# T5 bias sums of a two-layer decoder trunk on one core: nine packed sets of key groups in five breaks of the matmul row, in place of twelve sets in twelve breaks

## The chip, the core and the metric

The kernel runs on one core of one Trainium2 chip. The metric is the device time of one execution in microseconds (us), the median of three runs. TensorE (PE) does the matmuls, VectorE (DVE) and ScalarE (ACT) the elementwise work, GpSimd (POOL) a few small steps, and SyncE (SP) issues the weight DMAs. Each engine works through its own queue in order, and semaphores let one engine wait for another.

## The reference, cut to what matters

The program is a decoder trunk of two layers for 256 tokens of width 1024, in float32. Layer 0 is multi-head latent attention and layer 1 block-sparse attention with 8 heads; since there are only 256 tokens, layer 1 is plain causal attention over one block of 256 keys. Each attention is followed by a squared-ReLU MLP of width 4096. Layer 1 adds a bias that depends on the distance of query and key alone:

```python
def rel_bias(pq, pk):
    return table_h[h_i4, t5_bucket(pq - pk)].astype(jnp.float32)
...
lg_own = (jnp.einsum('bhqd,bhtd->bhqt', qi, k_own).astype(jnp.float32) * scale
          + rel_bias(pq4, pos_own[:, None, None, :]))
causal = (own * MOBA_BLOCK + t_ids)[None, :] <= q_idx[:, None]
parts.append(jnp.where(causal, lg_own, -jnp.inf))
```

Only pairs with the key not after the query count. For query tile 0 (queries 0 to 127) these are keys 0 to 127, for query tile 1 (queries 128 to 255) keys 0 to 255.

## The kernel before

**Matmul rows.** A float32 weight is split on the chip into a high and a low part (`wh` by an ACT cast, line 169, and `wl` by a DVE subtraction, line 178), and so are activations, and each product is three fp32r matmuls (`mm3`, line 87). The MLP of layer 0 runs two passes `r`; in each, places 0 to 7 (`first`) make hidden values and places 8 to 15 (`d` = 0 to 7) the output chunks. Every place is a chain of 48 matmuls of 256 columns into one PSUM bank. In this text places are counted through both passes, 0 to 31; pass 2 begins at 16 and its output chunks at 24. After place 31 come the projections of layer 1, whose first one, k0, goes through the input chunks k = 0 to 7 in order, six matmuls of 512 columns each, and needs the normalised input `hTh`, `hTl` of chunk k.

**The end of a pass-2 output chunk.** DVE scales the PSUM sum (line 976), POOL adds the residual `x` (line 1041; DVE for the last chunk), ACT makes `hTh` (line 609) and DVE `hTl` (line 611). Between these stand `wh` and `wl` of later weight units. All of it is in program order.

**Bias sums.** The bias is a sum over 32 thresholds: a step matrix `st` (is the query at least the key plus the threshold?), times a table of differences `parts3`. A `BiasBlock` handles a set of 32 keys of one query tile: `steps` is one DVE comparison that makes `st` in bf16 (line 1017), `sums` is eight bf16 matmuls with 96 columns into two PSUM banks, and `add` is six DVE additions (line 1034) that bring the sums to `bias`, the first of three on the causal mask `bias0` (the program's name for it is `mask`). There are twelve sets.

**What sets the order.** A hand-written list `fillers` names a place for each `steps` and each `add`; they go onto DVE's queue at the end of that place, ahead of the scaling in an output chunk. `inside` names the place whose matmul chain a `sums` breaks, five matmuls before its end. Set i has its comparison at place 2i+6 and its break and its additions at 2i+9, so breaks stand at 9, 11, ... 31. After a break the next chain begins with a matmul of 258 columns (`wider`). PSUM banks are taken in rotation from eight (`ps`, line 71). `bias_tables` at place 5 prepares the comparison's inputs; in the same place POOL finishes a sum of squares `ssum` (lines 301 and 306), which PE reads inside place 6.

Of the kernel before, what the change touches and what calls it, by code (L numbers as in the profile page):

```python
# [15 lines left out]
OP = mybir.AluOpType  # L16
AX = mybir.AxisListType

P = 128
# [7 lines left out]
H = 8  # L27
# [26 lines left out]
NPAIR = DFF // (2 * P * NR)  # L54
# [6 lines left out]
def trunk(ctx: ExitStack, tc: tile.TileContext, A, out):  # L61
    nc = tc.nc
# [8 lines left out]
    def ps():  # L71
        return psum.tile([P, 512], F32, name="ps", tag="ps")
# [5 lines left out]
    def t2(*shape):  # L78
        return work.tile([P, *shape], F32, name="t2", tag="t2")
# [4 lines left out]
    def mm(o, a, b, start, stop):  # L84
        nc.tensor.matmul(o, a, b, start=start, stop=stop)  # L85
# [21 lines left out]
    def other_type(i, f):  # L107
        def run():
            f()
            moved[0] = False  # L110
        return i, run
# [113 lines left out]
    for k in range(KD):  # L225
        if k > 1:
            load_one()
        if k < 4 or k % 2 == 0:
            n = 1 if k < 4 else 2
# [25 lines left out]
    bias0 = mask.rearrange("p a b -> p (a b)")  # L255
# [7 lines left out]
    def gain(name, i=0):  # L263
        return gains[:, GOFF[name][0] + i:GOFF[name][0] + i + 1]
# [21 lines left out]
    class SumSquares:  # L286


        def __init__(self):
            self.tot = work.tile([P, 2, S], F32, name="ssum", tag="ssum", bufs=1)  # L290
            self.prev = None

        def add(self, b, on_pool=False):
            sq = t2(2, S)
            xs = x[:, 2 * b:2 * b + 2]
            if on_pool:
                nc.gpsimd.tensor_mul(sq, xs, xs)
            else:
                nc.scalar.activation(sq, xs, AF.Square)
            if self.prev is not None:  # L300
                nc.gpsimd.tensor_add(self.tot, self.prev, sq)
                sq = self.tot
            self.prev = sq
# [532 lines left out]
    m = t2(NT, 2, PE_D)  # L836
# [13 lines left out]
    for o, a, b in rope_halves(m[:, :, 0], m[:, :, 1]):  # L850
        a, b = (i[:, :, None, :].to_broadcast([P, NT, 2, HALF]) for i in (a, b))
# [136 lines left out]
    bias = bias_pool.tile([P, H, 3 * P], F32)  # L988
    steps_q = bias_pool.tile([P, S], F32)
    steps_k = bias_pool.tile([P, S // 4], F32)  # L990
    parts3 = bias_pool.tile([P, 3 * 4 * H], BF16)

    def bias_tables():
        nc.vector.tensor_copy(steps_q, pos_row)
        nc.vector.tensor_copy(steps_k, pos_k4)
        nc.vector.tensor_scalar(steps_k, steps_k, gain("thr"), None, op0=OP.add)
        delta = bias_pool.tile([P, 4 * H], F32, name="delta")
        nc.vector.tensor_sub(delta, tprev.rearrange("p a b -> p (a b)"), tcur.rearrange("p a b -> p (a b)"))
        rest = delta
        for i in range(3):  # L1000
            pt = parts3[:, i * 4 * H:(i + 1) * 4 * H]
            nc.vector.tensor_copy(pt, rest)
            if i < 2:
                nxt = bias_pool.tile([P, 4 * H], F32, name=f"rest{i}")
                nc.vector.tensor_sub(nxt, rest, pt)
                rest = nxt

    class BiasBlock:


        def __init__(self, blk):
            self.t, self.k0 = (0, 32 * blk) if blk < 4 else (1, 32 * (blk - 4))

        def steps(self):
            t, k0 = self.t, self.k0
            self.st = bias_pool.tile([P, 8, P], BF16, name="st", tag="st", bufs=2)
            nc.vector.tensor_tensor(self.st, steps_q[:, None, t * P:(t + 1) * P].to_broadcast([P, 8, P]),
                                    steps_k[:, k0 // 4:k0 // 4 + 8, None].to_broadcast([P, 8, P]), op=OP.is_ge)

        def sums(self):  # L1020
            self.pb = [ps() for _ in range(2)]
            for h in range(2):
                for kk in range(4):
                    mm(self.pb[h][:, kk * 96:(kk + 1) * 96], self.st[:, 4 * h + kk], parts3, True, True)

        def add(self):
            col = self.k0 if self.t == 0 else P + self.k0
            for h in range(2):
                pb = self.pb[h]
                dst = bias[:, :, col + 16 * h:col + 16 * (h + 1)]  # L1030
                src = pb[:, :384].rearrange("p (k i g h) -> p i h k g", i=3, g=4, h=H)
                for i in range(3):
                    old = dst if i else bias0[:, None, col + 16 * h:col + 16 * (h + 1)].to_broadcast([P, H, 16])
                    nc.vector.tensor_tensor(dst.rearrange("p h (k g) -> p h k g", g=4), src[:, i],  # L1034
                                            old.rearrange("p h (k g) -> p h k g", g=4), op=OP.add)

    sums1 = [None]

# [11 lines left out]
        nc.vector.tensor_add(y, o, x[:, d])  # L1050
        (nc.sync if d == KD - 1 else nc.gpsimd).dma_start(out[:, d], y)

    blocks = [BiasBlock(i) for i in range(12)]
    inside = {}
    fillers = [((0, 1), table_loads), ((0, 5), bias_tables)]
    for i, b in enumerate(blocks):

        steps, place = (divmod(2 * i + g, 2 * NPAIR) for g in (6, 9))
        fillers += [(steps, b.steps), (place, b.add)]
        inside[place] = other_type(0, b.sums)  # L1060
    mlp(0, M0, fillers, inside, finish0)


# [150 lines left out]
```

## Time and profile before

| | |
|---|---|
| median of 3 runs | 564.68 us (564.36 to 564.85) |
| the profiled execution, its own time | 564.54 us |
| its span, first to last instruction | 562.7 us |
| PE busy | 554.5 us (99%) |
| DVE busy | 396.4 us (70%) |
| ACT busy | 302.8 us (54%) |
| POOL busy | 94.6 us (17%) |
| mean granted TensorE clock | 0.997 |

The profile is of one execution. Busy time of PE counts a matmul from start to modelled end, and matmuls overlap, so a full PE says only that work was always queued; the pace is read from the starts. The timeline gives the start, the duration and the idle time before an instruction with what ended it.

### The profile page before, as it was taken

Reading aid. Unit: us, or ns where it says so; the run is one execution under the profiler, and the core shown is the slowest. Engines: PE = TensorE matmul, PEld = TensorE weight load, DVE = VectorE, ACT = ScalarE, POOL = GpSimd, SP = SyncE. Lnnn points to the kernel's source line nnn. Section 1 sums busy time; section 2 is a strip of 40 time slices with the busy share of each in tenths; the row PEclk is TensorE's granted clock in tenths of the full one; section 3 lists DMA queues with packets and bytes.
Section 4 is the critical chain, followed back from the end, with each engine's and each line's share of the span. In section 5 each row is a group of like instructions: output and inputs, shape, how many; then the busy total and the mean of one; then the engine's idle time right before and its main releaser. Section 6 shows DMA issues by size and latency. Waiting matters only on the chain.

```text
span 562.7 us, 10806 instructions
## 1 busy us (share of the span) xinstructions
PE 554.5 (99%) x4346; PEld 527.3 (94%) x4346; DVE 396.4 (70%) x654; ACT 302.8 (54%) x495; POOL 94.6 (17%) x105
## 2 busy tenths in 40 slices
PE   8999999999999999999989999999999999999997
PEld 6878999999999999999868888999999999999997
DVE  5997777778987598766678466676876753877630
ACT  6989675665433356343455556646765332655420
POOL 4892100040232000011124100000130211000100
PEclk9999999999999999999989999999999999999999
DMA  8833444686675366544454553453775764575810
GB/s 299 296 123 118 146 139 158 187 280 190 188 223 189 112 217 196 176 155 157 152 182 123 186 191 115 147 181 113 230 224 181 251 201 150 159 219 185 265 45 29
DMA packets 29186, 99.57 MB, mean 177 GB/s; under 512 B 3824, under 2 KB 4720, under 8 KB 29136
## 3 DMA queue, kind: packets, MB, share of 16 engines
q1 hardware_dynamic: 28656, 97.94, 54.1%
q0 software_dynamic: 336, 0.92, 0.4%
q8 instruction: 34, 0.56, 0.4%
q14 instruction: 16, 0.13, 0.1%
q10 hardware_dynamic: 144, 0.02, 0.0%
HBM read 97.82 MB, written 1.05 MB: 176 GB/s over the span
## 4 chain that ended last, share of the span: by engine, by line
PE 95%; DVE 2%; DMA 1%; SPq 1%; issue 1%; POOL 0%; ACT 0%; DVEq 0%
PE ps L85 92%; PE ps L372 1%; PE ps L596 1%; DMA rowp<-in_rowp 1%; DVE wl L178 1%; SPq L158 0%; SPq L230 0%; DVE bias L1034 0%; POOL ang L393 0%; DVE hTl L280 0%; PE ps L512 0%; ACT wh L169 0%; POOL posf L391 0%; ACT hTh L609 0%; DVE x L1041 0%
## 5 line engine op out<-in xcount | busy, mean ns | idle before, releaser
L178 DVE TENSOR_TENSOR wl<-raw,wh 128x1024 fp32r<-128x1024 f32 x177 | 217.0, 1241 | 37.6 <-ACT wh L169 37.0
L169 ACT CAST wh<-raw 128x1024 fp32r<-128x1024 f32 x177 | 182.7, 1047 | 72.2 <-PE ps L85 53.6
L85 PE MATMUL ps<-a,wh 128*128 128x256 f32 x1024 | 175.3, 276 | 0.0
L85 PEld LDWEIGHTS ps<-a,wh 128*128 128x128 f32 x1024 | 154.4, 188 | 0.0
L85 PE MATMUL ps<-a,wl 128*128 128x256 f32 x512 | 142.1, 277 | 0.0
L85 PE MATMUL ps<-hTl,wh 128*128 128x256 f32 x512 | 141.7, 277 | 0.0
L85 PE MATMUL ps<-hTh,wl 128*128 128x256 f32 x512 | 141.7, 277 | 0.0
L85 PE MATMUL ps<-hTh,wh 128*128 128x256 f32 x512 | 141.3, 276 | 0.0
L85 PEld LDWEIGHTS ps<-hTl,wh 128*128 128x128 f32 x512 | 96.1, 188 | 0.1
L85 PEld LDWEIGHTS ps<-hTh,wh 128*128 128x128 f32 x512 | 96.1, 188 | 0.1
L85 PEld LDWEIGHTS ps<-a,wl 128*128 128x128 f32 x512 | 96.1, 188 | 0.0
L85 PEld LDWEIGHTS ps<-hTh,wl 128*128 128x128 f32 x512 | 96.1, 188 | 0.0
L930 ACT ACTIVATE t<-ps 128x512 f32<-128x512 f32 (+1 forms) x34 | 19.5, 572 | 67.5 <-PE ps L85 67.5
L85 PE MATMUL ps<-wh,hTh 128*128 128x512 f32 (+2 forms) x128 | 46.9, 392 | 3.7 <-ACT hTh L609 2.4
L85 PE MATMUL ps<-aT,wh 128*128 128x256 f32 (+1 forms) x256 | 50.4, 288 | 0.0
L932 DVE SCALAR_TENSOR_TENSOR t<-ps,t 128x512 f32<-128x512 f32 (+1 forms) x34 | 22.4, 659 | 38.4 <-ACT t L930 38.0
L85 PE MATMUL ps<-wl,hTh 128*128 128x512 f32 (+2 forms) x128 | 45.9, 384 | 0.2 <-DVE wl L178 0.2
L85 PE MATMUL ps<-wh,hTl 128*128 128x512 f32 (+2 forms) x128 | 45.7, 383 | 0.0
L85 PEld LDWEIGHTS ps<-aT,wh 128*128 128x128 f32 x256 | 40.3, 188 | 0.2
L609 ACT ACTIVATE hTh<-x,gains 128x256 fp32r<-128x256 f32 x24 | 12.2, 510 | 47.9 <-POOL x L1041 29.7
L85 PE MATMUL ps<-aT,wl 128*128 128x256 f32 x128 | 35.6, 278 | 0.0
L978 POOL TENSOR_TENSOR x<-t,x 128x256 f32<-128x256 f32 x16 | 19.4, 1211 | 93.4 <-DVE t L976 93.4
(166 smaller groups left out, 634.7 us busy)
## 6 DMA issues: line engine op xcount, KB each, us to landing
raw<-in_w_in_mlp SPq DMA_DIRECT2D x64, 512.0 KB, 4.1
raw<-in_w_out_mlp SPq DMA_DIRECT2D x64, 512.0 KB, 4.3
raw<-in_w_qkv SPq DMA_DIRECT2D x24, 512.0 KB, 4.2
raw<-in_w_u SPq DMA_DIRECT2D x8, 512.0 KB, 5.9
win<-in_w_in SPq DMA_DIRECT2D x8, 352.0 KB, 5.3
raw<-in_w_o0a SPq DMA_DIRECT2D x4, 512.0 KB, 3.6
raw<-in_w_o0b SPq DMA_DIRECT2D x4, 512.0 KB, 3.6
raw<-in_w_o1a SPq DMA_DIRECT2D x4, 512.0 KB, 3.8
```

Of the source, the lines that this page charges most:

```text
L85: nc.tensor.matmul(o, a, b, start=start, stop=stop)
L169: (eng.copy if eng is nc.scalar else eng.tensor_copy)(his[i][:, :w], raws[i][:, :w])
L178: eng.tensor_sub(los[i][:, :w], raws[i][:, :w], f32(his[i][:, :w]))
L372: nc.tensor.transpose(pt[:, i * P:(i + 1) * P], yf[:, i * P:(i + 1) * P], ident)
L596: nc.tensor.transpose(pt[:, i * P:(i + 1) * P], self.p[:, i * P:(i + 1) * P], ident)
L609: nc.scalar.activation(hTh[:, k], x[:, k], AF.Copy, scale=gain(gname, k))
L930: nc.scalar.activation(rl, src, AF.Relu)
L932: nc.vector.scalar_tensor_tensor(sq, src, 0.0, rl, op0=OP.max, op1=OP.mult)
L978: nc.gpsimd.tensor_add(x[:, d], y, x[:, d])
```

## The change

The six sets that hold a block on the causal diagonal need only some of their queries: of keys 96 to 127 in tile 0 the queries 96 to 127, and so on. The change packs two such sets into one `st` along the query columns: 32 columns of the one and 96 of the other, or 64 and 64. Three packed sets and six whole ones remain. A packed set has two comparisons (over fewer columns) and two groups of six additions, one for each part; the part that moves to other partitions writes 32 or 64 rows. Its rows that no sum reaches are filled from the mask by three POOL copies in `bias_tables`. Two sets share a break, so breaks stand at places 9, 14, 19, 24 and 29, with sixteen bf16 matmuls in the first four and eight in the last. Comparisons stand at 6, 7, 11, 12, 16, 17, 21, 22 and 26, groups of additions at 9, 10, 11, 14, 15, 16, 19, 20, 21, 24, 25 and 29.

```diff
     def bias_tables():
+        for q, k in ((96, 96), (64, 2 * P + 64), (96, 2 * P + 96)):
+            nc.gpsimd.tensor_copy(bias[:q, :, k:k + 32], bias0[:q, None, k:k + 32].to_broadcast([q, H, 32]))
         nc.vector.tensor_copy(steps_q, pos_row)
...
-        def __init__(self, blk):
-            self.t, self.k0 = (0, 32 * blk) if blk < 4 else (1, 32 * (blk - 4))
+        def __init__(self, *parts):
+            self.parts = [(slice(m, m + P - q0), t, k0, q0) for m, t, k0, q0 in parts]
...
+            for m, t, k0, q0 in self.parts:
+                n = P - q0
+                nc.vector.tensor_tensor(self.st[:, :, m],
+                                        steps_q[:, None, t * P + q0:(t + 1) * P].to_broadcast([P, 8, n]),
+                                        steps_k[:, k0 // 4:k0 // 4 + 8, None].to_broadcast([P, 8, n]), op=OP.is_ge)
...
+        def add(self, part):
+            m, t, k0, q0 = part
+            col = k0 if t == 0 else P + k0
+
+            if m.start == q0:
+                m, q0 = slice(0, P), 0
...
-    blocks = [BiasBlock(i) for i in range(12)]
+    whole = [BiasBlock((0, *p, 0)) for p in ((0, 0), (1, 0), (1, 32), (1, 64), (1, 96), (1, 128))]
+    packed = [BiasBlock((0, 0, 96, 96), (32, 0, 32, 32)), BiasBlock((0, 1, 224, 96), (32, 1, 160, 32)),
+              BiasBlock((0, 1, 192, 64), (64, 0, 64, 64))]
+    pairs = [(whole[i], packed[i]) for i in range(3)] + [(whole[3], whole[4]), (whole[5],)]
...
-        steps, place = (divmod(2 * i + g, 2 * NPAIR) for g in (6, 9))
-        fillers += [(steps, b.steps), (place, b.add)]
-        inside[place] = other_type(0, b.sums)
+    for i, bs in enumerate(pairs):
+        at = 5 * i + 9
+        place = divmod(at, 2 * NPAIR)
...
+        fillers += [(divmod(at - 3 + j, 2 * NPAIR), b.steps) for j, b in enumerate(bs)]
+        fillers += [(divmod(at + j, 2 * NPAIR), f) for j, f in enumerate(f for b in bs for f in b.adds())]
+        inside[place] = other_type(0, sums)
```

DVE's queue at the end of pass 2, from `hTl` of output chunk 5 to the residual of chunk 7 (`t` is the scaled chunk, `x` the residual); before:

```order
L611 SCALAR_TENSOR_TENSOR hTl<-x,gains,hTh 128x256
L178 TENSOR_TENSOR wl<-raw,wh 128x1024 x2
L976 TENSOR_TENSOR t_3617<-ps,scale 128x256
L611 SCALAR_TENSOR_TENSOR hTl<-x,gains,hTh 128x256
L178 TENSOR_TENSOR wl<-raw,wh 128x1024 x2
L1034 TENSOR_TENSOR bias<-ps,mask 128x8x16
L1034 TENSOR_TENSOR bias<-ps,bias 128x8x16 x2
L1034 TENSOR_TENSOR bias<-ps,mask 128x8x16
L1034 TENSOR_TENSOR bias<-ps,bias 128x8x16 x2
L976 TENSOR_TENSOR t_3699<-ps,scale 128x256
L1041 TENSOR_TENSOR x<-t_3699,x 128x256
```

The same place in the changed kernel:

```order
L611 SCALAR_TENSOR_TENSOR hTl<-x,gains,hTh 128x256
L178 TENSOR_TENSOR wl<-raw,wh 128x1024 x2
L976 TENSOR_TENSOR t_3603<-ps,scale 128x256
L611 SCALAR_TENSOR_TENSOR hTl<-x,gains,hTh 128x256
L178 TENSOR_TENSOR wl<-raw,wh 128x1024 x2
L976 TENSOR_TENSOR t_3669<-ps,scale 128x256
L1054 TENSOR_TENSOR x<-t_3669,x 128x256
```

The six additions ahead of the last chunk's scaling have left this place.

DVE's queue where the output chunks of pass 2 begin (`a` is the last hidden value), before:

```order
L940 TENSOR_TENSOR a_1322<-t_3081,a_1321 128x512
L178 TENSOR_TENSOR wl<-raw,wh 128x1024 x2
L1034 TENSOR_TENSOR bias<-ps,mask 128x8x16
L1034 TENSOR_TENSOR bias<-ps,bias 128x8x16 x2
L1034 TENSOR_TENSOR bias<-ps,mask 128x8x16
L1034 TENSOR_TENSOR bias<-ps,bias 128x8x16 x2
L178 TENSOR_TENSOR wl<-raw,wh 128x1024
L1017 TENSOR_TENSOR st<-steps_q,steps_k 128x1024
L976 TENSOR_TENSOR t_3160<-ps,scale 128x256
```

The same place in the changed kernel:

```order
L940 TENSOR_TENSOR a_1322<-t_3077,a_1321 128x512
L178 TENSOR_TENSOR wl<-raw,wh 128x1024 x3
L1044 TENSOR_TENSOR bias<-ps,mask 128x8x16
L1044 TENSOR_TENSOR bias<-ps,bias 128x8x16 x2
L1044 TENSOR_TENSOR bias<-ps,mask 128x8x16
L1044 TENSOR_TENSOR bias<-ps,bias 128x8x16 x2
L976 TENSOR_TENSOR t_3174<-ps,scale 128x256
```

Here the additions moved from place 23 to place 24, and the comparison of place 24 is gone.

POOL's queue around place 5, one piece of the difference (the sum of squares, which PE reads in place 6):

```order
 L301 TENSOR_TENSOR ssum<-ssum,t_1618 128x512
 L301 TENSOR_TENSOR ssum<-ssum,t_1688 128x512
+L996 COPY bias<-mask 96x8x32
+L996 COPY bias<-mask 64x8x32
+L996 COPY bias<-mask 96x8x32
 L306 TENSOR_TENSOR ssum<-ssum 128x256
```

The three copies stand ahead of the last step of the sum.

## Rows read from the trace of the kernel before

**Rows 1.** The page: busy time of the engines, and the chain of work that ended last, by engine.

```profile
PE 554.5 (99%) x4346; PEld 527.3 (94%) x4346; DVE 396.4 (70%) x654; ACT 302.8 (54%) x495; POOL 94.6 (17%) x105
...
PE 95%; DVE 2%; DMA 1%; SPq 1%; issue 1%; POOL 0%; ACT 0%; DVEq 0%
```

**Rows 2.** The waits of PE: for whom, us in total, times, longest.

```profile
PE ps L85 <- ACT hTh L609: 2.4, 1, 2.4
PE ps L85 <- DVE wh L446: 1.1, 1, 1.1
...
PE ps L85 <- DVE wl L178: 0.2, 1, 0.2
```

**Rows 3.** The timeline of PE around the break at place 9 and at the next one (start, duration, operation, count).

```profile
147.57 0.39 PE L85 MATMUL ps<-a,wh 128*128 128x256 f32 x2
147.81 0.51 PE L85 MATMUL ps<-parts,st 128*128 128x96 bf16 x8
148.14 0.37 PE L85 MATMUL ps<-a,wl 128*128 128x256 f32 x1
148.34 0.40 PE L85 MATMUL ps<-a,wh 128*128 128x256 f32 x2
...
148.94 0.28 PE L85 MATMUL ps<-a,wl 128*128 128x256 f32 x1
...
149.28 0.28 PE L85 MATMUL ps<-a,wl 128*128 128x256 f32 x1
...
159.15 0.51 PE L85 MATMUL ps<-parts,st 128*128 128x96 bf16 x8
```

**Rows 4.** The instructions on the tile `st`: count, shortest, median and longest duration in ns, first and last start.

```profile
L85 PE MATMUL ps<-parts,st x96: 206/206/217, 147.8 to 272.9; 128*128 128x96 bf16 x96
```

**Rows 5.** The timeline of PE in projection k0, where it waits for chunk 7; 13 matmuls start from 283.11 to 290.17, and the next at 290.60.

```profile
282.41 0.40 PE L85 MATMUL ps<-wl,hTh 128*128 128x512 f32 x1
...
283.11 0.39 PE L85 MATMUL ps<-wl,hTh 128*128 128x512 f32 x1
285.87 0.50 PE L85 MATMUL ps<-wh,hTh 128*128 128x512 f32 x1 [2.36 <-ACT hTh L609]
...
290.17 0.59 PE L85 MATMUL ps<-wl,hTh 128*128 128x512 f32 x1
290.60 0.40 PE L85 MATMUL ps<-wh,hTh 128*128 128x512 f32 x1
```

**Rows 6.** The view by windows around it: us, busy time (count) of PE, PEld, DVE, ACT and POOL, granted TensorE clock, DMA share, GB/s.

```profile
280.00:283.00 3.00, 3.00 (x15) 2.41 (x14) 2.56 (x3) 1.34 (x2) 0.00 (x0) 1.00 0.48 145
...
286.00:290.50 4.50, 4.48 (x12) 3.35 (x13) 3.52 (x4) 4.50 (x6) 2.90 (x2) 0.63 0.20 48
290.50:295.00 4.50, 4.50 (x22) 3.58 (x21) 2.36 (x4) 1.65 (x3) 0.00 (x0) 0.99 0.77 270
```

**Rows 7.** The timeline of DVE from the scaling of output chunk 6 to `hTl` of chunk 7.

```profile
277.67 0.41 DVE L976 TENSOR_TENSOR t<-ps,scale 128x256 f32<-128x256 f32 x1
...
280.42 2.36 DVE L178 TENSOR_TENSOR wl<-raw,wh 128x1024 fp32r<-128x1024 f32 x2 [0.46 <-ACT wh L169]
282.70 0.28 DVE L1034 TENSOR_TENSOR bias<-ps,mask 128x128 f32<-128x128 f32 x1
...
284.40 0.41 DVE L976 TENSOR_TENSOR t<-ps,scale 128x256 f32<-128x256 f32 x1
284.85 0.43 DVE L1041 TENSOR_TENSOR x<-t,x 128x256 f32<-128x256 f32 x1
285.85 0.48 DVE L611 SCALAR_TENSOR_TENSOR hTl<-x,gains,hTh 128x256 fp32r<-128x256 f32 x1 [0.58 <-ACT hTh L609]
```

**Rows 8.** Groups of DVE's instructions between the scaling of chunk 0 and that of chunk 7, 238.1 to 284.3 us: count | busy us, mean ns | idle us before them, and who ended it.

```profile
L1034 DVE TENSOR_TENSOR bias<-ps,bias 128x128 f32<-128x128 f32 x16 | 4.7, 291 | 0.6
L611 DVE SCALAR_TENSOR_TENSOR hTl<-x,gains,hTh 128x256 fp32r<-128x256 f32 x7 | 3.4, 484 | 10.2 <-ACT hTh L609 10.2
...
L1017 DVE TENSOR_TENSOR st<-steps_q,steps_k 128x1024 bf16<-128x1024 f32 x2 | 2.4, 1214 | 0.0
L1034 DVE TENSOR_TENSOR bias<-ps,mask 128x128 f32<-128x128 f32 x8 | 2.3, 281 | 0.0
```

**Rows 9.** The timeline of DVE from the additions of place 23 to the scaling of chunk 0 (place 24).

```profile
233.64 0.28 DVE L1034 TENSOR_TENSOR bias<-ps,mask 128x128 f32<-128x128 f32 x1
...
235.34 1.22 DVE L178 TENSOR_TENSOR wl<-raw,wh 128x1024 fp32r<-128x1024 f32 x1
236.47 1.22 DVE L1017 TENSOR_TENSOR st<-steps_q,steps_k 128x1024 bf16<-128x1024 f32 x1
237.60 0.42 DVE L976 TENSOR_TENSOR t<-ps,scale 128x256 f32<-128x256 f32 x1
```

**Rows 10.** The timeline of POOL: the last step of the sum of squares, and the residual of chunk 0 in pass 1.

```profile
126.67 0.74 POOL L306 TENSOR_TENSOR ssum<-ssum 128x256 f32<-128x256 f32 x1
147.81 1.65 POOL L978 TENSOR_TENSOR x<-t,x 128x256 f32<-128x256 f32 x1 [20.40 <-DVE t L976]
```

**Rows 11.** The timeline of PE in place 6, where it reads the sum of squares.

```profile
131.14 0.59 PE L85 MATMUL ps<-ssum,ones 128*128 128x256 f32 x2
```

**Rows 12.** Groups of POOL's instructions over the whole span, columns as in rows 8.

```profile
L415 POOL TENSOR_SCALAR rr<-rr 128x64 f32<-128x64 f32 x1 | 0.9, 893 | 0.1
...
L748 POOL MEMSET kpT<- 128x256 f32 x2 | 0.6, 312 | 0.0
```

More of the change, by code (lines that the diff above doesn't have):

```diff
@@ L1008, in trunk @@
     class BiasBlock:
-        def __init__(self, blk):
-            self.t, self.k0 = (0, 32 * blk) if blk < 4 else (1, 32 * (blk - 4))
+        def __init__(self, *parts):
+            self.parts = [(slice(m, m + P - q0), t, k0, q0) for m, t, k0, q0 in parts]
         def steps(self):
-            t, k0 = self.t, self.k0
             self.st = bias_pool.tile([P, 8, P], BF16, name="st", tag="st", bufs=2)
-            nc.vector.tensor_tensor(self.st, steps_q[:, None, t * P:(t + 1) * P].to_broadcast([P, 8, P]),
-                                    steps_k[:, k0 // 4:k0 // 4 + 8, None].to_broadcast([P, 8, P]), op=OP.is_ge)
+            for m, t, k0, q0 in self.parts:
[3 more added lines that the diff above has]
+                                        steps_k[:, k0 // 4:k0 // 4 + 8, None].to_broadcast([P, 8, n]), op=OP.is_ge)
         def sums(self):
@@ L1024, in sums, with adds @@
                     mm(self.pb[h][:, kk * 96:(kk + 1) * 96], self.st[:, 4 * h + kk], parts3, True, True)
-        def add(self):
-            col = self.k0 if self.t == 0 else P + self.k0
+        def add(self, part):
[3 more added lines that the diff above has]
+                m, q0 = slice(0, P), 0
             for h in range(2):
-                pb = self.pb[h]
-                dst = bias[:, :, col + 16 * h:col + 16 * (h + 1)]
-                src = pb[:, :384].rearrange("p (k i g h) -> p i h k g", i=3, g=4, h=H)
+                cols = slice(col + 16 * h, col + 16 * (h + 1))
+                dst = bias[q0:, :, cols]
+                src = self.pb[h][m, :384].rearrange("p (k i g h) -> p i h k g", i=3, g=4, h=H)
                 for i in range(3):
-                    old = dst if i else bias0[:, None, col + 16 * h:col + 16 * (h + 1)].to_broadcast([P, H, 16])
+                    old = dst if i else bias0[q0:, None, cols].to_broadcast([P - q0, H, 16])
                     nc.vector.tensor_tensor(dst.rearrange("p h (k g) -> p h k g", g=4), src[:, i],
                                             old.rearrange("p h (k g) -> p h k g", g=4), op=OP.add)
+        def adds(self):
+            return [lambda p=p: self.add(p) for p in self.parts]
     sums1 = [None]
@@ L1051, in finish1, with sums @@
         (nc.sync if d == KD - 1 else nc.gpsimd).dma_start(out[:, d], y)
-    blocks = [BiasBlock(i) for i in range(12)]
+    whole = [BiasBlock((0, *p, 0)) for p in ((0, 0), (1, 0), (1, 32), (1, 64), (1, 96), (1, 128))]
+    packed = [BiasBlock((0, 0, 96, 96), (32, 0, 32, 32)), BiasBlock((0, 1, 224, 96), (32, 1, 160, 32)),
+              BiasBlock((0, 1, 192, 64), (64, 0, 64, 64))]
+    pairs = [(whole[i], packed[i]) for i in range(3)] + [(whole[3], whole[4]), (whole[5],)]
     inside = {}
     fillers = [((0, 1), table_loads), ((0, 5), bias_tables)]
-    for i, b in enumerate(blocks):
-        steps, place = (divmod(2 * i + g, 2 * NPAIR) for g in (6, 9))
-        fillers += [(steps, b.steps), (place, b.add)]
-        inside[place] = other_type(0, b.sums)
+    for i, bs in enumerate(pairs):
+        at = 5 * i + 9
+        place = divmod(at, 2 * NPAIR)
+        def sums(bs=bs):
+            for b in bs:
+                b.sums()
+        fillers += [(divmod(at - 3 + j, 2 * NPAIR), b.steps) for j, b in enumerate(bs)]
+        fillers += [(divmod(at + j, 2 * NPAIR), f) for j, f in enumerate(f for b in bs for f in b.adds())]
+        inside[place] = other_type(0, sums)
     mlp(0, M0, fillers, inside, finish0)
```

## The prediction

> **What bounds the kernel now.** I read the page first. PE is busy for 99% of the span and carries 95% of the chain that ended last [rows 1], so a change counts in two ways only: it takes work out of PE's row, or it takes away a wait of PE. The waits come next. The longest is 2.36 us, in projection k0, for `hTh` of chunk 7 [rows 2, 5]. Then I read PE's pace in the timeline. Around the breaks it is even: three matmuls of 256 columns start every 0.34 us (148.94 to 149.28) [rows 3]. At the wait it is not: the matmuls of 512 columns started every 0.23 us (282.41 to 283.11 is three), and behind the wait they come to 0.43 us apart (290.17 to 290.60) [rows 5]. The windows say why: the granted clock is 1.00 up to 283 us, that is 2.4 GHz, 0.63 as a mean from 286.00 to 290.50, so for most of that stretch PE ran at the lower level, 1.2 GHz, and 0.99 behind it [rows 6]. What the engine did before the fall was to wait.
>
> The wait ends the layer-0 MLP, and the DVE timeline shows who is late. The scaling of chunk 7 starts at 284.40, straight after six bias additions that began at 282.70 [rows 7]. PE had finished all eight chunks long before: k0 wants chunk 7 after 42 of its matmuls, so it began 9.8 us before 283.34, at 273.5. So the end of pass 2 is set by DVE's queue, not by PE, though DVE is busy for only 70% of the span.
>
> **The change part by part.**
>
> *Fewer matmuls and breaks.* From one break to the next (147.81 to 159.15) are 11.34 us, and in them lie 96 matmuls of the row and one break [rows 3]. The 96 alone take 32 x 0.34 = 10.88, so a break with eight bf16 matmuls costs 0.46. The eight themselves take 0.33 (147.81 to 148.14) [rows 3]; the other 0.13 is the slower restart (148.14 to 148.34 for one matmul) and belongs to the break, however many sets it holds. Before: 12 x 0.46 = 5.52. After: nine sets x 0.33 + five breaks x 0.13 = 3.62. All of it is on PE's row, so **1.90 us** go, 1.0 of it by the three sets and 0.9 by the seven breaks. The 206 ns that the tile view gives for one bf16 matmul [rows 4] is latency, not pace: eight would be 1.65 by it, and the row moves on after 0.33.
>
> The Trainium skill (TensorE: Matmul & The Clock Gate, Back-to-back issue gap) gives about 81 ns as the sustained spacing of load-and-matmul pairs at 128 columns. By that, as an estimate, 24 pairs fewer would be worth 1.94 instead of 1.0 and the time would be 557.4; the trace has 41 ns at 96 columns, so I keep the trace's.
>
> *DVE at the end of pass 2.* From place 23 on, before, the list puts five groups of additions (23, 25, 27, 29, 31) and three comparisons (24, 26, 28); after, three groups (24, 25, 29) and one comparison (26). A group takes 1.70 (282.70 to 284.40) [rows 7], a comparison 1.13 (236.47 to 237.60) [rows 9]. So 2 x 1.70 + 2 x 1.13 = 5.66 us leave DVE's queue ahead of the scaling of chunk 7. Do they bring it forward by as much? Between the two scalings DVE's idle time is the wait for `hTh`, 10.2 us in seven times [rows 8], and that wait follows DVE's own scaling by POOL's residual and ACT's cast: it moves along with DVE. The scaling of chunk 7 then starts at 284.40 - 5.66 = 278.74.
>
> PE restarted 1.47 after that scaling (284.40 to 285.87) [rows 5, 7]. Without a wait it would have started at 283.11 + 0.23 = 283.34, so the scaling must start by 281.87. In the changed kernel PE also comes earlier, relative to the start of the output chunks: four breaks (25, 27, 29, 31), 1.84, stood between, and now two (24 with two sets, 29), 0.79 + 0.46 = 1.25. The deadline is then 281.28, and DVE is there at 278.74, **2.5 us ahead**. The wait goes.
>
> What it is worth is more than its idle time: from 283.11 to 290.60 are 7.49 us for 13 matmuls that take 13 x 0.233 = 3.03 at the full clock [rows 5]. So **4.46 us** go, some 2.5 of wait and 1.9 of slow matmuls. What is late next? Chunk 6 is wanted 1.4 us before chunk 7 (six matmuls) and its scaling runs over 5 us before (277.67 against 284.40, less the 1.70 additions) [rows 7], so it has more room. Projections and heads behind k0 show no wait of PE; the sequence there (k0's sums, the sum of squares, the roots) is started by PE itself and moves with it.
>
> *Where DVE's work goes.* The additions stay twelve groups of six; the packed sets' comparisons have the same 1024 columns in two instructions, so at most one more start-up each, and three whole comparisons (3.4 us) are gone. In places 9 to 22 it comes in lumps: places 16 and 21 now hold a group and a comparison, 2.8 us. What is delayed there is `wl` of later units and the hidden values. The cover is the units split ahead: at the end of pass 2 DVE's queue stood 11 us behind PE, and in the whole span PE waited 0.2 us for `wl` [rows 2], so 2.8 are hidden. If that cover were gone, each of the two lumps would cost at most its 2.8. I take nothing. The additions for 32 or 64 rows are not in the trace; between nothing (fewer rows) and 1.70 a group (same columns) I take 1.70, the row with the same columns, and it does not reach PE either way.
>
> *POOL's copies.* Three copies of 256 elements stand ahead of the last step of the sum of squares, which PE reads at 131.14 [rows 11]; that step ends at 126.67 + 0.74 = 127.41 [rows 10], so 3.73 us are free. No row shows such a copy. The floor is a fill of 256 elements, 0.31; the ceiling is a row of 64 elements at 0.89, four times that 3.6 [rows 12]. I take 0.74, the row of two inputs and 256 elements in that very place [rows 10]: 2.2 us, hidden. DVE loses a little to them, on work that has slack.
>
> *Sum.* 1.90 + 4.46 = 6.36, from 564.54 for the profiled execution 558.2; the median of the runs lies 0.14 above it, so **558.3 us**.
>
> **The rivals.**
>
> *The wait shrinks but leaves the slow stretch.* If DVE gains 3 us less than counted (ACT's casts pacing it, or lumps carried in from place 21), PE still waits briefly, and the clock may fall as before: 4.46 - 2.5 = 1.9 come back, giving 560.3, and up to 562 with a wait of a microsecond or two. For it: the margin is 2.5 only. Against it: the idle time of DVE there is tied to its own steps [rows 8].
>
> *Only PE's row gets shorter.* If the end of pass 2 is paced by POOL and ACT, not by DVE's fillers, the wait stays: 564.7 - 1.9 = 562.8. Against it: the scaling of chunk 7 follows the additions at once [rows 7].
>
> *Slower: POOL's copies hold up PE in place 6.* PE is in order, so a late sum of squares stops the whole row. At 1.65 a copy (the residual with the same 256 elements beside DVE's work [rows 10]) the sum would end at 126.67 + 4.95 + 0.74 = 132.4, a wait of 1.2, with the clock's 1.9 behind it: 561.4, still faster. It decides from 2.7 us a copy on: 3 x 2.7 - 3.73 = 4.4 of wait and 1.9 of slow matmuls eat up the 6.36. At the ceiling of 3.6 the wait is 7.1, and 558.3 + 7.1 + 1.9 = 567.3. Rows 10 bear on it: the same size took 0.74 and 1.65. The Trainium skill (SBUF, Who interferes with whom) says that a DVE instruction with two SBUF inputs and a GpSimd instruction that reads SBUF exclude each other for a whole instruction. As an estimate by that, with one `wl` of 1.22 [rows 9] waited out per copy, the sum ends 5.9 later, a wait of 2.2, and the time is 562.4; the two rows agree that something of the kind happens.
>
> *It does not do what it says: the second set of a pair is not ready.* A break now takes four banks and two `st` at once. If a bank were still held by additions in DVE's queue, PE would wait for about one group, 1.70, in four breaks: 6.8, so 565.1, no change, or with slow stretches up to 568. Against it: eight banks are rotated, a place takes one, five places stand between breaks, and both comparisons are queued at least two places ahead.
>
> **How the numbers follow.** Chances: forecast 0.70; shrunk wait 0.11; row alone 0.07; POOL 0.06, half of it slower than before; second set late 0.06, half no change, half slower. About 0.2%, 1.1 us, is what a measurement of this kernel can tell from no change. Faster: 0.70 + 0.11 + 0.07 + 0.03 = 0.91; same 0.03; slower 0.06. The forecast itself spans 557.5 to 559.2 (the runs differ by 0.5, the terms by a few tenths); up to 561.6 the range takes in most of the shrunk wait and POOL at 1.65, together 0.8.
>
> **What would show it.** Right: sixteen bf16 matmuls in a row at about 41 ns apart, breaks about 28 us apart (five places of 5.44 and one break of 0.79); no wait of PE for `hTh` in k0 and a granted clock of 1.00 through the stretch behind it; scaling of chunk 7 some 6 us after k0 begins instead of 11; PE's `ssum` matmul not waiting. Wrong: a wait left in k0 with a clock below 1, a gap in PE's row at place 6, or one ahead of a second set of bf16 matmuls.

## The result and the profile after

| | before | after |
|---|---|---|
| median | 564.52 us, 4 runs (562.97 to 564.85) | 558.72 us, 4 runs (558.56 to 558.94) |
| ratio after to before | | 0.9900, 95% interval 0.9881 to 0.9918 |
| the profiled execution, its own time | 564.54 us | 558.83 us |
| its span | 562.7 us | 557.0 us |

The changed kernel is 5.8 us faster. The forecast was 558.3, with a range of 557.5 to 561.6.

The page of the changed kernel, as [rows 1] of before: busy time and the chain that ended last.

```profile
PE 552.0 (99%) x4322; PEld 526.8 (95%) x4322; DVE 395.0 (71%) x654; ACT 303.4 (54%) x495; POOL 93.2 (17%) x108
...
PE 98%; DMA 1%; DVE 0%; issue 0%; SPq 0%
```

PE has 24 matmuls fewer, and its share of the chain rose from 95% to 98%: the 2% that DVE had in it are gone. DVE's total hardly moved (396.4 to 395.0), so the amount of DVE's work in the whole program can't have made the difference. Whether its place did is what the experiments test.

All waits of PE in the changed kernel, as [rows 2].

```profile
PE ps L85 <- DVE warm L218: 1.0, 1, 1.0
PE ps L85 <- DVE wh L446: 0.6, 1, 0.6
```

Both lie at the start of the program. The wait for `hTh` is not there, nor one for `wl`.

PE's timeline around the first break and at the next one, as [rows 3], and across chunk 7 in k0, as [rows 5].

```profile
148.46 0.85 PE L85 MATMUL ps<-parts,st 128*128 128x96 bf16 x16
149.13 0.37 PE L85 MATMUL ps<-a,wl 128*128 128x256 f32 x1
149.34 0.40 PE L85 MATMUL ps<-a,wh 128*128 128x256 f32 x2
...
176.46 0.85 PE L85 MATMUL ps<-parts,st 128*128 128x96 bf16 x16
...
281.92 0.39 PE L85 MATMUL ps<-wl,hTh 128*128 128x512 f32 x1
282.15 0.40 PE L85 MATMUL ps<-wh,hTh 128*128 128x512 f32 x1
```

Sixteen bf16 matmuls take 0.67 (148.46 to 149.13), 42 ns each, and the first matmul behind them takes 0.21 until the next starts. Breaks are 28.00 us apart. The instructions on the tile `st`, as [rows 4], say that there are 72 now, and no longer or shorter each than before:

```profile
L85 PE MATMUL ps<-parts,st x72: 206/206/217, 148.5 to 260.8; 128*128 128x96 bf16 x72
```

In k0 the matmul at 282.15 is the first that needs chunk 7, and it follows 0.23 behind the one before.

The windows of that stretch, columns as in [rows 6].

```profile
280.00:283.00 3.00, 3.00 (x14) 2.41 (x14) 2.00 (x3) 3.00 (x4) 2.27 (x2) 1.00 0.61 225
283.00:286.00 3.00, 3.00 (x15) 2.41 (x14) 3.00 (x4) 2.38 (x4) 0.62 (x1) 1.00 0.59 168
286.00:290.50 4.50, 4.50 (x23) 3.71 (x22) 1.36 (x4) 1.65 (x2) 0.37 (x1) 1.00 0.72 243
```

The granted clock is 1.00 throughout, 2.4 GHz, and 23 matmuls fit into the last window instead of 12.

DVE's timeline ahead of chunk 7, as [rows 7].

```profile
273.54 0.41 DVE L976 TENSOR_TENSOR t<-ps,scale 128x256 f32<-128x256 f32 x1
...
276.29 2.36 DVE L178 TENSOR_TENSOR wl<-raw,wh 128x1024 fp32r<-128x1024 f32 x2 [0.46 <-ACT wh L169]
278.57 0.42 DVE L976 TENSOR_TENSOR t<-ps,scale 128x256 f32<-128x256 f32 x1
```

The scaling of chunk 7 follows the two `wl` at once and starts 6.2 us after k0 began (272.36), not 10.85 as before.

**Where the 5.7 us between the two executions came from**, read from PE's starts at the borders of the stages:

| stage of PE's row | before | after | difference |
|---|---|---|---|
| up to the first MLP matmul of layer 0 | 93.51 | 94.16 | +0.65 |
| MLP of layer 0, to the first matmul of k0 | 180.04 | 178.20 | -1.84 |
| k0, to the first matmul of q0 | 14.49 | 11.19 | -3.30 |
| from there to the MLP of layer 1 | 96.72 | 95.54 | -1.18 |
| MLP of layer 1, to its last matmul | 174.43 | 174.42 | -0.01 |

The sum is -5.68, and the spans differ by 5.68. The first line lies ahead of all that was changed. In the profiled executions of the experiments below this start lies anywhere between 93.31 and 94.56, so it belongs to the execution and not to the change.

### The profile page after: what moved, and what is told of

Its sections match the earlier page's. It is cut to its first block, busy times and chain, and to the rows that moved or that the text cites. A ratio compares the mean times of both kernels' runs of the same rounds, so it can differ in the third digit from the quotient of the medians.

```text
span 557.0 us, 10752 instructions
## 1 busy us (share of the span) xinstructions
PE 552.0 (99%) x4322; PEld 526.8 (95%) x4322; DVE 395.0 (71%) x654; ACT 303.4 (54%) x495; POOL 93.2 (17%) x108
## 4 chain that ended last, share of the span: by engine, by line
PE 98%; DMA 1%; DVE 0%; issue 0%; SPq 0%
PE ps L85 96%; PE ps L372 2%; PE ps L596 1%; DMA win<-in_w_in 1%; PE ps L512 0%; DVE t L1063 0%; SPq L230 0%; DVE wh L446 0%; PE ps L879 0%
## 5 line engine op out<-in xcount | busy, mean ns | idle before, releaser
L178 DVE TENSOR_TENSOR wl<-raw,wh 128x1024 fp32r<-128x1024 f32 x177 | 219.2, 1255 | 35.0 <-ACT wh L169 34.5
```

What stands on the lines that cost most here:

```text
L178: eng.tensor_sub(los[i][:, :w], raws[i][:, :w], f32(his[i][:, :w]))
```

## The experiments

The first group asks which part of the change paid, the second what DVE's margin and PE's wait are worth, the third what a break holds.

**Twelve sets, only earlier.** The kernel before, with its twelve breaks and comparisons, but with the sets 1.5 places apart instead of 2, so that nothing of them is left at the end of pass 2:

```diff
-        steps, place = (divmod(2 * i + g, 2 * NPAIR) for g in (6, 9))
+        steps, place = (divmod(3 * i // 2 + g, 2 * NPAIR) for g in (6, 9))
```

> The kernel before, with its twelve sets in twelve breaks, but set i has its break at place 9 + 3i/2 (9, 10, 12, 13, ... 24, 25) instead of 9 + 2i; no packing and no shared break. Theory (two terms: less work in PE's row, and DVE's queue relieved at the end of pass 2): the row keeps its twelve breaks (5.5 us), but from place 23 on DVE has two groups of additions and no comparison instead of five and three, 8.5 us less, so the wait of PE in k0 and the slow matmuls behind it go: 564.5 - 4.5 = 560.1, no wait for hTh. Rival (the packing and the shared breaks are what counts, the wait is not set by DVE's additions): the wait stays, 564.5.

Measured: 560.38 us (median of ten runs; the seven at the usual pace lie between 559.57 and 560.66, and the other three, at 567.4 to 567.7, among them the profiled one, are told of at the end), ratio 0.9952 (0.9911 to 0.9993). PE's timeline at chunk 7:

```profile
283.69 0.39 PE L85 MATMUL ps<-wl,hTh 128*128 128x512 f32 x1
283.92 0.40 PE L85 MATMUL ps<-wh,hTh 128*128 128x512 f32 x1
```

The scaling of chunk 7 in DVE's timeline, 4.9 behind the start of k0 (274.13):

```profile
279.07 0.42 DVE L976 TENSOR_TENSOR t<-ps,scale 128x256 f32<-128x256 f32 x1
```

No wait is left, though no set was packed and no break saved. The MLP row of layer 0 takes 180.06 from start to end, as before (180.04), and k0 takes 11.19, as after. So some 4.5 us (564.44, the median of the kernel before in the same series among executions under 566, to 559.98, the median of the seven) come from *when* the sets are worked off. By PE's row the packing and the pairing hold another 1.86 (180.06 here, 178.20 in the changed kernel); by the medians 1.3 are left for them.

**The five pairs two places later.** The packed and paired sets, moved back to where their additions meet the last chunk again:

```diff
-        at = 5 * i + 9
+        at = 5 * i + 11
```

> The changed kernel with every pair two places later (breaks at 11, 16, 21, 26, 31 instead of 9 to 29); the same nine sets and five breaks. Theory: from place 23 on DVE has four groups of additions and three comparisons instead of three and one, 1.70 + 2.26 = 4.0 us more, so the scaling of chunk 7 comes at about 282.5 where PE needs it by 280.7: a wait of 1.8 us in k0 is back, 560.6 if the clock stays up, 562.5 if it falls again behind the wait. Rival (the row alone): 558.7, no wait.

Measured: 560.67 us (560.10 to 561.01), ratio 0.9932 (0.9916 to 0.9949). DVE's timeline ahead of the wait:

```profile
281.00 0.61 DVE L1044 TENSOR_TENSOR bias<-ps,bias 128x128 f32<-128x128 f32 x2
281.54 0.41 DVE L976 TENSOR_TENSOR t<-ps,scale 128x256 f32<-128x256 f32 x1
```

PE's timeline of the same kernel at the wait:

```profile
281.06 0.39 PE L85 MATMUL ps<-wl,hTh 128*128 128x512 f32 x1
283.00 0.50 PE L85 MATMUL ps<-wh,hTh 128*128 128x512 f32 x1 [1.55 <-ACT hTh L609]
283.53 0.50 PE L85 MATMUL ps<-wh,hTl 128*128 128x512 f32 x1
283.86 0.39 PE L85 MATMUL ps<-wl,hTh 128*128 128x512 f32 x1
284.09 0.40 PE L85 MATMUL ps<-wh,hTh 128*128 128x512 f32 x1
```

The same work at a later place brings the wait back: the additions stand right ahead of the scaling again, and PE restarts 1.46 behind it, as it did in the kernel before (1.47). Behind this wait of 1.55 the row is back at 0.23 a matmul after two slower ones; the clock stayed up.

**More work on DVE ahead of chunk 6.** One, three or five additional comparisons at place 30, with a result that nothing reads:

```diff
+    junk = bias_pool.tile([P, 8, P], BF16, name="junk")
+
+    def more():
+        for _ in range(N):
+            nc.vector.tensor_tensor(junk, steps_q[:, None, :P].to_broadcast([P, 8, P]),
+                                    steps_k[:, :8, None].to_broadcast([P, 8, P]), op=OP.is_ge)
+
+    fillers += [(divmod(30, 2 * NPAIR), more)]
```

One: 

> The changed kernel with one more comparison on DVE at place 30 (1.13 us). Theory: it fits into the 2.1 us by which the scaling of chunk 7 comes before PE needs it: no wait in k0, 558.7. Rival (DVE is still what sets the end of pass 2): 559.8.

Three: 

> The changed kernel with three more comparisons on DVE at place 30, into a tile that nobody reads (3 x 1.13 = 3.4 us of DVE, nothing on PE). Theory: the scaling of chunk 7 moves from 278.6 to 282.0, 1.3 us behind the time by which PE needs it: 560.0 with the clock up, 561.9 with the clock down behind the wait. Rival (DVE's queue has more room than reckoned, or the wait does not hang on it): 558.7.

Five: 

> The changed kernel with five more comparisons on DVE at place 30 into a tile that nobody reads (5 x 1.13 = 5.65 us). Theory: the scaling of chunk 7 is 3.5 us late: a wait of 3.5 in k0, 562.2 with the clock up, 564.1 with it down behind the wait; the fall of the clock belongs to the longer waits, not to this place of the program. Rival (the clock falls for another reason in the kernel before, such as the break at place 31 just ahead of k0): no fall, 562.2 in every run.

| comparisons | time, us | scaling of chunk 7 after k0's start | PE's wait for `hTh` |
|---|---|---|---|
| 0 (the changed kernel) | 558.72 | 6.21 | 0 |
| 1 | 558.54 (558.28 to 558.63) | 7.37 | 0 |
| 3 | 560.20 (nine of ten from 559.80 to 560.88, one at 567.81) | 9.88 | 1.41 |
| 5 | 564.22 (563.01 to 565.38) | 12.37 | 0.63 and 2.72 |

The ratios are 0.9894 (0.9879 to 0.9909), 0.9944 (0.9915 to 0.9973) and 1.0000 (0.9987 to 1.0014). One comparison fits into the margin, three do not, and five eat up the whole gain, with all the packing and pairing still there. PE's timeline with five:

```profile
282.78 0.39 PE L85 MATMUL ps<-wl,hTh 128*128 128x512 f32 x1
285.89 0.80 PE L85 MATMUL ps<-wh,hTh 128*128 128x512 f32 x1 [2.72 <-ACT hTh L609]
...
287.00 0.63 PE L85 MATMUL ps<-wl,hTh 128*128 128x512 f32 x1
287.43 0.63 PE L85 MATMUL ps<-wh,hTh 128*128 128x512 f32 x1
```

The window behind it, columns as in [rows 6]:

```profile
287.00:290.50 3.50, 3.50 (x12) 2.79 (x11) 3.18 (x3) 3.21 (x5) 2.38 (x2) 0.69 0.43 125
```

Matmuls of 512 columns start 0.43 apart and the granted clock is 0.69 as a mean: for most of that window it is the lower level, 1.2 GHz, as in [rows 5] and [rows 6]. With three, behind 1.41 us of wait, they were 0.23 apart again from the third one on. Every execution is listed with the mean granted clock of its span. It is 0.999 or 1.000 in all ten with three and in all four of the pairs placed later; with five it is 0.994 to 0.997 in nine of ten, and 1.000 in the one that took 563.01.

**The kernel before once more**, for a second profile of its wait.

> The kernel before, unchanged, profiled once more. The waits of 1.4 and 1.6 us in k0 that two kernels showed left the granted clock at 1.00, and the times of the kernel before lie in two bunches, about 562.9 and 564.8. Theory: the wait of 2.4 us is there in every execution, the lower clock behind it only in some, and is worth 1.9 us: a profile either with the clock down behind the wait and 564.2 to 565.3, or with the clock up and 562.4 to 563.2. Rival (the bunches come from elsewhere, say the start): the clock falls in every execution, whichever bunch it is in.

Measured: ten runs with a median of 564.45, four of them at 562.80 to 563.15 and six at 564.42 to 565.19. The profiled execution is one of the first four, 563.15. PE's timeline at the wait:

```profile
286.08 0.50 PE L85 MATMUL ps<-wh,hTh 128*128 128x512 f32 x1 [2.40 <-ACT hTh L609]
286.60 0.50 PE L85 MATMUL ps<-wh,hTl 128*128 128x512 f32 x1
286.93 0.40 PE L85 MATMUL ps<-wl,hTh 128*128 128x512 f32 x1
287.17 0.39 PE L85 MATMUL ps<-wh,hTh 128*128 128x512 f32 x1
```

The window behind it, columns as in [rows 6]:

```profile
286.00:290.50 4.50, 4.40 (x18) 3.36 (x19) 3.47 (x3) 4.50 (x7) 2.91 (x2) 1.00 0.15 49
```

The same wait of 2.4, and here the clock stayed at 1.00. So the fall that [rows 6] show comes in some executions and not in others, and the rival, a fall in every execution, is out. From the start of k0 to the MLP of layer 1 this execution takes 109.67 and the first one 111.21, so the fall costs 1.5 there. That the two bunches of times are the two clocks is seen in the list of all executions of the kernel before: of those that took less than 566 us, 41 have a mean granted clock of 0.997 and took 563.81 to 565.38 (median 564.91), and 21 have 1.000 and took 562.30 to 563.69 (median 562.99). The bunches are 1.9 apart; the two profiles show 1.5 of it.

**The sets one by one.** The changed kernel, with the second set of a pair in a break of its own at the next place (nine breaks):

```diff
-        place = divmod(at, 2 * NPAIR)
...
-        inside[place] = other_type(0, sums)
+        for j, b in enumerate(bs):
+            inside[divmod(at + j, 2 * NPAIR)] = other_type(0, b.sums)
```

> The changed kernel with its nine sets unpaired: the second set of a pair breaks the row one place later (breaks at 9, 10, 14, 15, 19, 20, 24, 25, 29); DVE's order as in the changed kernel. Theory (a break costs 0.13 us by itself, a set 0.33): four breaks more, +0.5 us: 559.2, each break 0.46. Rival (the cost hangs on the sets alone): 558.7, no difference in the row.

Measured: 558.85 us (nine of ten runs from 558.33 to 559.20; the tenth, the profiled one, at 566.50, is told of at the end), ratio 0.9921 (0.9889 to 0.9954). That can't be told from the changed kernel by the time. By the trace, the MLP row of layer 0 takes 178.68 instead of 178.20: four breaks more cost 0.48, 0.12 each, so a break has a price of its own.

**Three breaks.** Nine sets in three breaks of three, with the comparisons three places ahead or fewer, as the pairs have them:

```diff
-            self.st = bias_pool.tile([P, 8, P], BF16, name="st", tag="st", bufs=2)
+            self.st = bias_pool.tile([P, 8, P], BF16, name="st", tag="st", bufs=3)
...
-    pairs = [(whole[i], packed[i]) for i in range(3)] + [(whole[3], whole[4]), (whole[5],)]
+    pairs = [(whole[0], packed[0], packed[1]), (whole[1], whole[2], packed[2]), tuple(whole[3:])]
...
-        at = 5 * i + 9
+        at = 7 * i + 9
```

> The changed kernel with its nine sets in three breaks of three (places 9, 16, 23), and three st buffers instead of two. Theory: two breaks fewer at 0.12 each, 0.25 us, no wait in k0, DVE's queue relieved by one group and one comparison more at the end of pass 2: 558.5, which the times can hardly tell from 558.7 but PE's row can. Rival (six banks at once are too many): PE waits at a break or two chains behind it, 559 or more.

Measured: 561.98 us (561.59 to 562.58), ratio 0.9956 (0.9944 to 0.9969), 3.3 more than the changed kernel, where the expectation was 0.2 less. Behind the start of the program PE has one wait in the list, for `st`, 0.2. PE's timeline at the first and the third break:

```profile
147.74 1.44 PE L85 MATMUL ps<-parts,st 128*128 128x96 bf16 x24
149.00 0.36 PE L85 MATMUL ps<-a,wl 128*128 128x256 f32 x1
...
228.92 0.51 PE L85 MATMUL ps<-parts,st 128*128 128x96 bf16 x8 [0.19 <-DVE st L1022]
```

DVE's comparison for the third set of the first break:

```profile
147.32 1.28 DVE L1022 TENSOR_TENSOR st<-steps_q,steps_k 128x256 bf16<-128x256 f32 x2
```

Windows of 20 us behind the first, the second and the third break, columns as in [rows 6]:

```profile
151.00:171.00 20.00, 20.00 (x173) 20.00 (x172) 18.19 (x37) 7.36 (x7) 6.60 (x4) 1.00 0.70 214
205.00:225.00 20.00, 20.00 (x179) 20.00 (x178) 18.90 (x31) 11.61 (x16) 0.00 (x0) 1.00 0.66 199
232.00:252.00 20.00, 20.00 (x172) 20.00 (x172) 14.85 (x30) 8.27 (x11) 1.48 (x2) 1.00 0.43 132
```

In the first break the third set's comparison ends at 148.60, inside the break, whose 24 matmuls take 1.26 (147.74 to 149.00). Both delays are a small part of the loss. The rest is pace (the rival, six banks too many, expected a longer wait and not this): behind the two breaks in which a set was late, 173 and 172 matmuls of 256 columns fit into 20 us, and behind the second one, where all were ready, 179, all at a granted clock of 1.00. A slow matmul takes 0.117 to 0.118 us from start to start and a quick one 0.113 to 0.114. The MLP row of layer 0 takes 181.72.

**Three breaks with the comparisons one place earlier.** The same, so that no set is late:

```diff
-        fillers += [(divmod(at - 3 + j, 2 * NPAIR), b.steps) for j, b in enumerate(bs)]
+        fillers += [(divmod(at - 4 + j, 2 * NPAIR), b.steps) for j, b in enumerate(bs)]
```

> The kernel with three breaks of three sets (561.98), with each comparison one place earlier and nothing else changed, so that the third st of a break is ready when PE comes to it. In that kernel PE waited 0.2 us for st inside the first and the third break, and the matmuls behind those two breaks started every 0.117 to 0.118 us until the next break, against 0.113 to 0.114 behind the second, where no wait stood. Theory (a wait inside the bf16 matmuls costs the row its pace until the next break, some 3 us, and six banks at once cost nothing): no wait, 0.34 us for three matmuls everywhere, 558.5. Rival (24 bf16 matmuls or three sets in one break are themselves what costs the pace): the pace is lost again and the time stays at 562.

Measured: 558.08 us (557.72 to 558.74, six runs), ratio 0.9887 (0.9871 to 0.9903). PE's timeline at the first break:

```profile
148.60 1.19 PE L85 MATMUL ps<-parts,st 128*128 128x96 bf16 x24
149.62 0.37 PE L85 MATMUL ps<-a,wl 128*128 128x256 f32 x1
```

The windows behind the first and the third:

```profile
151.00:171.00 20.00, 20.00 (x179) 20.00 (x178) 18.89 (x38) 7.97 (x8) 6.11 (x4) 1.00 0.72 220
...
232.00:252.00 20.00, 20.00 (x179) 20.00 (x178) 14.76 (x30) 7.09 (x9) 1.80 (x3) 1.00 0.44 140
```

With the sets ready, 24 bf16 matmuls take 1.02 instead of 1.26, and the pace is the quick one behind both breaks that had lost it. The MLP row takes 177.95, 0.25 less than with five breaks and 3.77 less than with a late set. By the medians it is 0.6 quicker than the changed kernel, more than the row explains, but the ranges overlap.

**The matmul of 258 columns.** The changed kernel with `wider` giving 256 columns, here and wherever else it is called:

```diff
-        return bank[:, :S + 2], flat(b[:, :2])[:, :S + 2]
+        return bank[:, :S], flat(b[:, :2])[:, :S]
```

> The changed kernel with the matmul of 258 columns behind a break put back to 256 columns, everywhere (also behind the sum of squares at place 6 and in the attention). Theory: behind a break the matmuls start every 0.117 to 0.118 us until one of 258 columns has come, six of them in the changed kernel; without it the slower pace stays to the end of the layer-0 MLP, some 1300 matmuls from place 6 on at 0.004, about 5 us: 564, and more if the layer-1 MLP is slow too. Rival (the pace comes back by itself): 558.7.

Measured: 572.66 us (572.59 to 573.00), ratio 1.0147 (1.0129 to 1.0165): 13.9 us slower than the changed kernel, for some matmuls of two columns fewer, and 8.7 more than the theory had without a slow MLP of layer 1. Two windows of this kernel (us, busy time and count of PE, granted clock, DMA share, GB/s):

```profile
100.00:120.00 20.00, 20.00 (x172) 1.00 0.66 216
400.00:420.00 20.00, 20.00 (x172) 1.00 0.75 236
```

The first of them in the changed kernel:

```profile
100.00:120.00 20.00, 20.00 (x178) 1.00 0.71 227
```

Both MLPs run at the slow pace, that of layer 0 from its first place on and not only from place 6: their rows take 184.83 and 181.22 instead of 178.20 and 174.42, 13.4 more together, with no wait in either and the clock at 1.00. The rival, that the pace comes back by itself, is out.

## Why the prediction was right

**PE's row, 1.90 forecast: 1.84 measured.** The split into 0.33 a set and 0.13 a break holds: sixteen matmuls take 0.67, and the nine breaks put 0.12 on each of the four more. Only what the 0.13 is made of was misread. The prediction put it on one matmul and called the pace around a break even; the restart is 0.20 instead of 0.113, and the next matmuls start 0.116 to 0.121 apart until one behind that of 258 columns (148.34 to 148.94 holds five, 0.12 each). The spacing of the bf16 matmuls is 42 ns. The Trainium skill (TensorE: Matmul & The Clock Gate, Back-to-back issue gap) has about 81 ns for pairs of 128 columns; at 96 columns the trace has half of it, and the gain by the page, an estimate, would have been about 1 too large here.

**The wait in k0 and the slow matmuls behind it, 4.46: 3.30 + 1.18 = 4.48 measured.** Twelve sets placed earlier win this part alone; five pairs placed later, or three comparisons put in, lose about 2 us of it, and five comparisons all of it. That the end of pass 2 hung on the place of DVE's fillers, and not on how many sets there are, is thus shown from both sides. The rival "only PE's row gets shorter" (562.8) falls with it.

**The margin, 2.5: 2.1 measured.** PE needs the scaling 1.47 before 282.15, at 280.68, and has it at 278.57. PE's side of the reckoning was exact; DVE's was 0.45 too good. Between the scalings of chunk 0 and chunk 7 DVE gained 4.52, against 2 x 1.70 + 1.13 = 4.53 counted there; but the comparison that left the queue ahead of chunk 0 brought 0.69 and not 1.13. DVE's timeline shows the missing 0.44, first after, then before:

```profile
227.71 1.22 DVE L1022 TENSOR_TENSOR st<-steps_q,steps_k 128x1024 bf16<-128x1024 f32 x1
```

```profile
229.03 0.69 DVE L932 SCALAR_TENSOR_TENSOR t<-ps,t 128x512 f32<-128x512 f32 x1 [0.85 <-ACT t L930]
```

After, the comparison of place 22 is run only when place 24 has begun, behind the lump of place 21, and the squares behind it (line 932) start at 228.85, 1.27 after that place begins at 227.58. Before, DVE stood idle there, and the squares start 0.83 after the place begins (228.20). So a lump was carried in from place 21, of which the rival with a shrunk wait spoke. Two rows of the table above agree with a margin of about 2: one comparison more is free, and three (3.67 later) leave a wait of 1.41.

**The 1.9 of slow matmuls** was the term with the least behind it: I took it from one execution, as if the wait always brought it. The second profile of the kernel before shows the wait without the fall: then only the two matmuls behind the wait are slower (0.52 and 0.33 instead of 0.23), 0.4 of the 1.9, and from k0 to the MLP of layer 1 the change is worth 109.67 - 106.73 = 2.94 instead of 4.48. The median of before lies with the executions in which the clock fell, and in this term it was luck that the sum came out right; against the others the gain is 562.98 - 558.72 = 4.3.

**The rival with a shrunk wait** (560.3 to 562) named a real point 2.1 us away, and the kernels with pairs placed later and with three comparisons have such a wait: 560.7 and 560.2, near its lower end, but not by its mechanism. They waited longer than it had for 560.3, 1.4 to 1.55, and the clock stayed up.

**POOL's copies, 0.74 each: 0.39 measured.** POOL's timeline around them, as [rows 10]:

```profile
127.19 1.08 POOL L996 COPY bias<-mask 96x256 f32<-96x256 f32 x3
128.23 0.73 POOL L306 TENSOR_TENSOR ssum<-ssum 128x256 f32<-128x256 f32 x1
```

PE's reading of the sum, as [rows 11]:

```profile
131.79 0.59 PE L85 MATMUL ps<-ssum,ones 128*128 128x256 f32 x2
```

The sum ends at 128.96, 2.8 ahead of PE. A copy with one input was nearer to the fill of 0.31 than to the step with two. Whether the copies and a `wl` would shut each other out, as the Trainium skill (SBUF — State Buffer, Who interferes with whom) leads one to expect, stays open: no `wl` ran beside them in this execution. The next `wl`, which starts at 128.57 inside the last step of the sum, took 1.48; before, it started behind that step and took 1.23. That is one row each, and no run tested it.

**Additions for fewer rows, taken as 1.70 a group,** cost the same as whole ones. Groups of DVE's instructions in the changed kernel, columns as in [rows 8]:

```profile
L1044 DVE TENSOR_TENSOR bias<-ps,bias 128x128 f32<-128x128 f32 x36 | 10.5, 291 | 1.2
...
L1044 DVE TENSOR_TENSOR bias<-ps,bias 32x128 f32<-32x128 f32 x8 | 2.3, 283 | 0.3
```

So packing two sets saves matmuls and comparisons, and no additions. The lumps at places 16 and 21 cost PE no wait for a `wl`, as taken; the second shows in DVE's margin, as said above.

**The rival with a late second set** was priced at 1.70 a break, a group of additions that holds a bank. With five breaks no set was late. With three breaks the third set was late in two of them, and that cost 3.3 us; but the price was not a wait (0.2). It was the pace of everything up to the next break or the end of the MLP, which no row of before that I read would have told.

**What was missed** is 0.4 us of the median and 0.6 of the profiled execution. The later start (+0.65) covers it in the profiled one; that it does in the median is likely and not shown.

## What to carry to other kernels

When a filler on an engine that is 70% busy is moved, look for the stage whose last consumer waits, count what stands in that engine's queue between the previous deadline and this one, and give the distance to the deadline as a number: here it was 2.1 us, and the gain was all there with one comparison more and gone with five. Before a cheaper way to do small work is put down as the gain, place the old work differently and measure that: here it had over three quarters of it (4.5 of 5.8). When several small jobs share a break of a matmul row, have all their inputs ready a place earlier than the order seems to need, since a late one can cost many times its own wait (here 3.3 us for a wait of 0.2).

## What the runs showed of the hardware that was not expected

**A row of fp32r matmuls has two paces at one granted clock.** A matmul of 256 columns starts every 0.113 to 0.114 or every 0.117 to 0.118 us, 179 or 172 in 20 us, with PE 100% busy, no wait and the clock at 1.00. In the changed kernel the slow pace stands behind its first break too, but only up to the matmul of 258 columns at 149.81; from the second one behind that the quick pace is back. Without any matmul of 258 columns both MLPs ran at the slow pace throughout. Such a matmul does not always bring the quick pace back. In the first three-break kernel one stands behind each break with a late set (149.67 and 229.93; waits of 0.07 and 0.19 among the bf16 matmuls), and the pace stayed slow to the next break or to the end of the MLP; with the sets ready, the same matmuls brought it back. What in TensorE holds this state is open; it was not tried to change the pace by anything but these columns and the readiness of the sets.

**The same pace explains two profiled executions that are 7 us longer.** The profiled one of the twelve early sets (567.74) runs its MLP of layer 1 at the slow pace from the first matmul on, without a wait or a lower clock, though a matmul of 258 columns stands ahead of it at 372.68:

```profile
400.00:420.00 20.00, 20.00 (x172) 1.00 0.72 223
```

That MLP takes 181.22 there, to the hundredth what it takes without the 258 columns, and 174.42 otherwise. The same holds for the profiled execution of nine breaks (566.50). What brings the slow pace in there is open, since no late set and no wait stands near; that the other long executions (567.4 to 567.8) are of this kind is likely and not shown, as they have no profile. The two MLP rows of layer 0 and the k0 that are given above from those two profiles lie ahead of it.

**The clock does not answer a wait in the same way each time.** Behind waits of 1.41 and 1.55 us it stayed at 2.4 GHz in the profiled executions, and the mean of no other execution of those two kernels is below 0.999; behind 2.36 it fell to 1.2 GHz in one profile and behind 2.40 it stayed up in another; behind 0.63 and 2.72, in one projection, it fell. One and the same kernel has both: 0.997 in 41 executions of the kernel before and 1.000 in 21.
